# The first feed-forward product as seven block products of sums, in a hybrid diffusion block on one Trainium2 core

## The chip, the cores and the metric

One core of a Trainium2 chip runs the whole program once. The metric is the device time of that one execution in microseconds (us). Before the change it is 974.69 us, the median of 3 runs (974.1 to 976.0). The engines are TensorE (PE, with its weight loads shown as a row of its own, PEld), VectorE (DVE), ScalarE (ACT), GpSimd (POOL) and SyncE (SP), which here only issues transfers.

## The reference

One layer over 512 latent tokens of width 1024, with 256 context tokens. Three mixers run on the same normalised input, are merged by gates and projected back; then comes a SwiGLU feed-forward part with `D_FF = 2816`, and a last normalisation. The change concerns the product `h @ w_ffn_in`, of 512x1024 by 1024x5632.

```python
def swiglu(h, w_ffn_in, w_ffn_out):
    a, b = split_cols(h @ w_ffn_in, (D_FF, D_FF))
    return (jax.nn.silu(a) * b) @ w_ffn_out

x = x + g2 * swiglu(modulate(x, norm2_g[layer], sh2, sc2), w_ffn_in[layer], w_ffn_out[layer])
return rmsnorm(x, final_g)
```

## The kernel before

All products are done in a split form. An fp32 operand is rounded to fp32r on ACT (`A.copy`, L143) and the rest is taken on DVE (`V.tensor_tensor` subtract, L144); a product of two split operands is then three matmuls, high by high, high by low and low by high (`mm3`, L255 to L257). Every weight block of 128x1024 numbers (512 KB) is loaded by SP into one of three buffers `wf` (`load_w`, L139), and split into one of two buffer pairs `wh`, `wl` (`prep_w`). So a pair comes free only when the matmuls of two blocks earlier are done, and a buffer `wf` only when its split is done.

The order of each engine's instructions is fixed when the program is built: a scheduler takes the instructions by priority (weight loads and splits have the priority "prep", ahead of "main") and by its own estimate of when they can start. On the chip each engine runs its list strictly in that order, and waits at the first instruction whose inputs or buffers are not ready.

The last part of the kernel has three stages.

1. The product with `w_o` (`gemm_tm`, L985). It runs over token tiles m = 0 to 3 of 128 tokens, and as each tile's sums finish, the loop around it (L1028 and on) adds the residual (L1008), squares and sums (L1009), scales the row (L1030), transposes the tile in 8 blocks on PE (L1037), applies scale and shift (half of the blocks on DVE at L1043, half on ACT at L1041) and splits the result into `h2h`, `h2l`, features on partitions and tokens along the row. So the second normalisation of the last tiles lies beside the first matmuls of the next stage.
2. The first feed-forward product, 11 groups of 256 columns of `a` and the same 256 columns of `b`. Group 0 is done in two halves of 256 tokens, so that it can start before tokens 256 to 511 are there (192 matmuls of 256 columns). Groups 1 to 10 have 96 matmuls each, of 512 columns. `silu(a)` is done on ACT (L1082), the product with `b` on DVE (L1083), and the result is split at once into `Ga`, `Gb`.
3. The product with `w_ffn_out`, `gemm_tm` again over 22 blocks of 128 weight rows, each first multiplied by the gate `g2b` (L154), with the last normalisation behind it.

PSUM has eight banks of 512 fp32 columns: three `g`, one `t`, four `d`.

Of the kernel before, what the change touches and what calls it, by code (L numbers as in the profile page):

```python
# [9 lines left out]
F32 = mybir.dt.float32  # L10
# [64 lines left out]
def body(tc, I, out):  # L75
# [3 lines left out]
    with es:  # L79
# [22 lines left out]
        def gbank(name="g"):  # L102
            return psg.tile([128, 512], F32, name=name, tag="g")
# [708 lines left out]
        def cvf():  # L812
            return pF.tile([128, 512], F32, name="cvf", tag="cv", bufs=3)
# [212 lines left out]
        h2h = pH.tile([128, 8, 512], F32R, name="h2h", tag="hh")  # L1026
        h2l = pH.tile([128, 8, 512], F32R, name="h2l", tag="hl")
        for m, ps in gemm_tm(I["w_o"][0], g1b, lambda k, ms: (mh[:, k, ms], ml[:, k, ms]), 8, extra, 1):  # L1028
            rs_ = residual(ps, xr, m, [xn[:, m % 2, 512 * n:512 * n + 512] for n in range(2)])
            V.tensor_scalar(out=xn[:, m % 2], in0=xr[:, m], scalar1=rs_, scalar2=None, op0=ALU.mult)  # L1030
            for k4 in range(2):
                px = dbank()
                hf = cvf()
                p3, h3 = (t.rearrange("p (k j) -> p k j", k=4) for t in (px, hf))
# [9 lines left out]
                ms = slice(128 * m, 128 * m + 128)  # L1044
                split(h3, h2h[:, 4 * k4:4 * k4 + 4, ms], h2l[:, 4 * k4:4 * k4 + 4, ms])
        fstack.close()


        pG = es.enter_context(tc.tile_pool(name="pG", bufs=1))
        Ga = pG.tile([128, 18, 2, 512], F32R, name="Ga")  # L1050
        Gb = pM.tile([128, 4, 2, 512], F32R, name="Gb", tag="M16")
        Gt = [Ga[:, k] for k in range(18)] + [Gb[:, k] for k in range(4)]
        gw = pM.tile([128, 2, 2, 4, 256], F32R, name="gw", tag="C16")
        wfi = I["w_ffn_in"][0].rearrange("(k p) f -> p k f", p=128)
        H2 = (lambda k: h2h[:, k], lambda k: h2l[:, k], 512, gbank)
        cvg = lambda: pG.tile([128, 512], F32, name="cvg", tag="cv", bufs=3)
        for g in range(11):
            if g == 0:

                ab = [[gbank() for _ in range(2)], [gbank(), tbank()]]  # L1060
                wts = []
                for i in range(2):
                    for half in range(2):
                        dst = None
                        if i:
                            dst = [gw[:, half, p] for p in range(2)]
                        wts.append(prep_w(load_w(wfi[:, 4 * half:4 * half + 4, 2816 * i:2816 * i + 256]), dst=dst))
                for th in range(2):
                    ts = slice(256 * th, 256 * th + 256)
                    for i in range(2):  # L1070
                        for q in range(2):
                            cs = slice(128 * q, 128 * q + 128)
                            for k in range(8):
                                wh, wl = wts[2 * i + k // 4]
                                mm3(ab[i][q][:, ts], wh[:, k % 4, cs], wl[:, k % 4, cs], h2h[:, k, ts], h2l[:, k, ts], k == 0, k == 7)
                pa_, pb_ = ab
# [3 lines left out]
            for q in range(2):  # L1080
# [9 lines left out]
        for m, ps in gemm_tm(I["w_ffn_out"][0], g2b, lambda k, ms: (Gt[k][:, 0, ms], Gt[k][:, 1, ms]), 22, extra):  # L1090
            yo = yos[:, m]
            rs_ = residual(ps, xr, m, [cvg() for _ in range(2)])
# [19 lines left out]
```

## Time and profile before

| | before |
|---|---|
| median of 3 runs | 974.69 us |
| the profiled execution | 969.97 us, of it span 968.2 us |
| TensorE busy | 952.9 us, 98% of the span, 5964 matmuls |
| VectorE busy | 543.2 us, 56% |
| ScalarE busy | 421.8 us, 44% |
| GpSimd busy | 28.8 us, 3% |
| read from HBM | 110.58 MB, 118 GB/s over the span |

The profile is of one execution; its times are read as durations of single instructions and as the distance between the starts of neighbours. Matmuls are pipelined: one lasts longer than the distance to the next, so the distance between starts is what a matmul costs in a stream. A wait in brackets behind a row is the idle time of the engine ahead of it and what ended it.

### The profile page before, as it was taken

Reading aid. Unit: us, or ns where it says so; the run is one execution under the profiler, and the core shown is the slowest. Engines: PE = TensorE matmul, PEld = TensorE weight load, DVE = VectorE, ACT = ScalarE, POOL = GpSimd, SP = SyncE. Lnnn points to the kernel's source line nnn. Section 1 sums busy time; section 2 is a strip of 40 time slices with the busy share of each in tenths; the row PEclk is TensorE's granted clock in tenths of the full one; section 3 lists DMA queues with packets and bytes.
Section 4 is the critical chain, followed back from the end, with each engine's and each line's share of the span. In section 5 each row is a group of like instructions: output and inputs, shape, how many; then the busy total and the mean of one; then the engine's idle time right before and its main releaser. Section 6 shows DMA issues by size and latency. Waiting matters only on the chain.

```text
span 968.2 us, 14628 instructions
## 1 busy us (share of the span) xinstructions
PE 952.9 (98%) x5964; PEld 785.1 (81%) x5964; DVE 543.2 (56%) x880; ACT 421.8 (44%) x733; POOL 28.8 (3%) x47
## 2 busy tenths in 40 slices
PE   8999999999999999999999999999999999999997
PEld 7587888777888888888778888988888888888885
DVE  3575888379755333787874977333333333444455
ACT  5363985597773333362234346322323232311224
POOL 1002300000000000000000000000000000000000
PEclk9999999999999999999999999999999999999999
DMA  9820553421202323847765252223232332333322
GB/s 330 292 66 3 144 131 88 132 67 34 67 2 66 109 88 84 291 131 267 253 219 174 91 172 66 66 87 109 88 107 88 99 98 91 91 102 98 97 88 87
DMA packets 96836, 115.30 MB, mean 119 GB/s; under 512 B 18124, under 2 KB 84032, under 8 KB 96768
## 3 DMA queue, kind: packets, MB, share of 16 engines
q1 hardware_dynamic: 88192, 109.01, 35.7%
q0 software_dynamic: 1632, 3.44, 1.4%
q10 hardware_dynamic: 6944, 1.91, 0.8%
q8 instruction: 47, 0.77, 0.3%
q14 instruction: 21, 0.17, 0.1%
HBM read 110.58 MB, written 3.77 MB: 118 GB/s over the span
## 4 chain that ended last, share of the span: by engine, by line
PE 83%; DVE 6%; ACT 5%; DMA 4%; issue 2%; POOL 0%; SPq 0%; DVEq 0%; ACTq 0%
PE g L256 19%; PE g L257 19%; PE g L255 19%; PE d L255 5%; PE d L256 5%; PE d L257 5%; DMA wm<-in_w_mod_dram 2%; DVE acc L835 1%; DVE wl L144 1%; PE t L257 1%; PE t L255 1%; PE t L256 1%; PE d L238 1%; ACT TBD L639 1%; DMA acc<-in_b_mod_dram 1%
## 5 line engine op out<-in xcount | busy, mean ns | idle before, releaser
L144 DVE TENSOR_TENSOR wl<-wf,wh 128x1024 fp32r<-128x1024 f32 x131 | 160.1, 1222 | 205.0 <-ACT wh L143 204.1
L143 ACT CAST wh<-wf 128x1024 fp32r<-128x1024 f32 x131 | 137.8, 1052 | 309.9 <-PE g L256 169.6
L257 PE MATMUL g<-hh,wl 128*128 128x512 f32 x368 | 146.0, 397 | 0.3 <-DVE wl L144 0.3
L255 PE MATMUL g<-hh,wh 128*128 128x512 f32 x368 | 146.1, 397 | 0.0
L256 PE MATMUL g<-hl,wh 128*128 128x512 f32 x368 | 145.9, 396 | 0.0
L255 PE MATMUL g<-h2h,wh 128*128 128x512 f32 (+1 forms) x352 | 133.6, 380 | 0.0
L257 PE MATMUL g<-h2h,wl 128*128 128x512 f32 (+1 forms) x352 | 133.5, 380 | 0.0
L256 PE MATMUL g<-h2l,wh 128*128 128x512 f32 (+1 forms) x352 | 133.5, 379 | 0.0
L257 PEld LDWEIGHTS g<-hh,wl 128*128 128x128 f32 x368 | 69.6, 189 | 15.0 <-DVE wl L144 1.0
L256 PEld LDWEIGHTS g<-hl,wh 128*128 128x128 f32 x368 | 69.6, 189 | 13.7 <-issue 0.2
L255 PEld LDWEIGHTS g<-hh,wh 128*128 128x128 f32 x368 | 69.6, 189 | 13.6 <-issue 0.2
L255 PEld LDWEIGHTS g<-h2h,wh 128*128 128x128 f32 x352 | 66.2, 188 | 12.6
L256 PEld LDWEIGHTS g<-h2l,wh 128*128 128x128 f32 x352 | 66.2, 188 | 12.6
L257 PEld LDWEIGHTS g<-h2h,wl 128*128 128x128 f32 x352 | 66.1, 188 | 12.3
L154 DVE TENSOR_TENSOR wf<-wf,g2b 128x1024 f32<-128x1024 f32 x22 | 27.0, 1226 | 54.3 <-DMA wf<-in_w_ffn_out_dram 54.2
L835 DVE SCALAR_TENSOR_TENSOR acc<-wm,ct,acc 128x1024 f32<-128x1024 f32 x32 | 41.0, 1282 | 17.5 <-DMA acc<-in_b_mod_dram 8.0
L255 PE MATMUL d<-wh,Ga 128*128 128x512 f32 x72 | 28.0, 389 | 0.0
L256 PE MATMUL d<-wl,Ga 128*128 128x512 f32 x72 | 28.0, 389 | 0.0
L257 PE MATMUL d<-wh,Ga 128*128 128x512 f32 x72 | 28.0, 389 | 0.0
L718 ACT ACTIVATE SJ<-SJ,eGl 128x128 f32<-128x128 f32 x80 | 25.1, 402 | 3.8 <-PE d L706 2.6
L143 ACT CAST Ga<-cvg 128x512 fp32r<-128x512 f32 x18 | 11.1, 619 | 25.4 <-DVE cvg L1083 25.4
L616 DVE TENSOR_TENSOR t<-W 128x30 f32<-128x30 f32 (+29 forms) x60 | 19.3, 322 | 3.7 <-issue 2.7
(467 smaller groups left out, 1712.0 us busy)
## 6 DMA issues: line engine op xcount, KB each, us to landing
wm<-in_w_mod_dram SPq DMA_DIRECT2D x48, 512.0 KB, 5.3
wf<-in_w_ffn_in_dram SPq DMA_DIRECT2D x44, 512.0 KB, 3.5
wf<-in_w_in_dram SPq DMA_DIRECT2D x31, 512.0 KB, 3.9
wf<-in_w_gate_dram SPq DMA_DIRECT2D x24, 512.0 KB, 3.8
wf<-in_w_ffn_out_dram SPq DMA_DIRECT2D x22, 512.0 KB, 3.5
wf<-in_w_o_dram SPq DMA_DIRECT2D x8, 512.0 KB, 3.6
xl<-in_x_dram SPq DMA_DIRECT2D x4, 512.0 KB, 5.1
wf<-in_w_sc_out_dram SPq DMA_DIRECT2D x4, 512.0 KB, 3.3
```

Source lines behind the costliest of these rows:

```text
L143: A.copy(out=hi, in_=f)
L144: V.tensor_tensor(out=lo, in0=f, in1=hi.bitcast(F32), op=ALU.subtract)
L154: V.tensor_tensor(out=w, in0=w, in1=scale, op=ALU.mult)
L238: T.matmul(pm[32 * j:32 * j + 32, n * i:n * i + n], lhsT=ct[:, k, :], rhs=w[:, kk, :], start=k < 4, stop=k >= 4, tile_position=(0, 32 * j))
L255: T.matmul(ps, lhsT=lh, rhs=rh, start=start, stop=False)
L256: T.matmul(ps, lhsT=lh, rhs=rl, start=False, stop=False)
L257: T.matmul(ps, lhsT=ll, rhs=rh, start=False, stop=stop)
L616: V.tensor_tensor(out=t, in0=W3[0:n, j + 1:, j:j + 1].broadcast_to(sh_), in1=W3[0:n, j:j + 1, 0:j].broadcast_to(sh_), op=ALU.mult)
L639: A.copy(out=TBD[qs, slot, :, 32 * q:32 * q + 32], in_=Sy[qs])
L718: A.activation(out=S[:, u ^ par, h], in_=S[:, u ^ par, h], func=AF.Copy, scale=eGl[:, u, c_:c_ + 1])
L835: V.scalar_tensor_tensor(out=acc, in0=w, scalar=ct[:, k, 0:1], in1=acc, op0=ALU.mult, op1=ALU.add)
```

## The change

The 2x2 block product of a group of columns is done with seven products instead of eight. The weight of a group is cut into four blocks (`wsrc(i, half, g)`: i = 0 for `a`, 1 for `b`; half for features 0 to 511 and 512 to 1023), the tokens into two halves of 256. Seven sums of weight blocks meet seven sums of blocks of `h`, and the four results (`a` and `b`, for each half of the tokens) are sums of the products. The scheme of before had, in the same units, eight products.

- Each product (`prod`) is 24 matmuls of 256 columns: two column tiles, four feature blocks, three matmuls of the split form.
- The sums of `h` are made once, behind the second normalisation (`sums_b`, and `T4` at L1140), and are split like `h` before.
- The sums of weights are made for each group: one block is loaded by SP into a buffer of its own (`t` in `pre`, `w` in `ws`, two of each), a second block is added by a transfer of POOL's queue that accumulates into it (`acc_w`, L1113), and two more blocks are added on DVE (`add_w`, L1117). So a group issues seven transfers of 512 KB (five of SP, two of POOL) where it had four.
- In the groups a third split pair (`third`, shown as `w3`) is used in turn with `wh`, `wl`, so a split can start when the product of three places earlier is done (`prep3`).
- The results of a group are put together on DVE (`u2`, `e57`, `c22`, `c12`, `c21`, then two products with `silu`), with two copies and two `silu` on ACT. `G` is kept in fp32 (`Gq`), and split only when the second product comes to it (`g_of`).
- For groups 0 to 2 the two products that need only the first half of the tokens (`ahead` with `B11`, `ahead2` with `B21`) are put ahead of everything else, 144 matmuls in six products.

```diff
+        def prod(bank, w, b, first, last):
+            for q in range(2):
+                o, cs = bank[:, 256 * q:256 * q + 256], slice(128 * q, 128 * q + 128)
+                for kk in range(4):
+                    mm = ((w[0], b[:, 0]), (w[0], b[:, 1]), (w[1], b[:, 0]))
+                    for i, (l_, r_) in enumerate(mm):
+                        T.matmul(o, lhsT=l_[:, kk, cs], rhs=r_[:, kk], start=first and q == kk == i == 0,
+                                 stop=last and kk == 3 and i == 2, skip_group_check=True)
+        def acc_w(w, src):
+            with prio("prep"):
+                GP.dma_start(out=w, in_=src, accum_op=ALU.add)
+        def add_w(w, other):
+            with prio("prep"):
+                V.tensor_tensor(out=w, in0=w, in1=other, op=ALU.add)
...
+            for h, js in parts:
+                V.tensor_tensor(out=Bf[:, 0:4, js], in0=h[0], in1=Bf[:, 0:4, js], op=ALU.subtract)
+                split_b(Bf[:, 0:4, js], "T1", js)
...
+        def ahead(g, e):
+            X = gbank()
+            prod(X, prep_w(load_w(wsrc(0, 0, g))), OB["B11"], True, False)
+            A.copy(out=e, in_=X)
+            return X
+        def ahead2(g, X):
+            prod(X, prep_w(load_w(wsrc(0, 1, g))), OB["B21"], False, True)
...
+        EARLY = 3
+        Xs = [ahead(g, e1s[g]) for g in range(EARLY)]
+        for g in range(EARLY):
+            ahead2(g, Xs[g])
+        V.tensor_tensor(out=Bf[:, 4:8], in0=Bf[:, 4:8], in1=Bf[:, 0:4], op=ALU.subtract)
+        split_b(Bf[:, 4:8], "T4", slice(0, 256))
...
         for g in range(11):
-            if g == 0:
...
-                (pa_,) = gemm_fm(wfi[:, :, 256 * g:256 * g + 256], (H2,))
-                (pb_,) = gemm_fm(wfi[:, :, 2816 + 256 * g:2816 + 256 * g + 256], (H2,))
-            for q in range(2):
-                sa = cvg()
-                A.activation(out=sa, in_=pa_[q], func=AF.Silu)
-                V.tensor_tensor(out=sa, in0=pb_[q], in1=sa, op=ALU.mult)
-                split(sa, Gt[2 * g + q][:, 0], Gt[2 * g + q][:, 1])
+            t, w = pre[g % 2], ws[g % 2]
+            load_w2(wsrc(1, 0, g), t)
+            acc_w(t, wsrc(1, 1, g))
+            load_w2(wsrc(0, 0, g), w)
+            acc_w(w, wsrc(1, 0, g))
+            v = load_w(wsrc(0, 0, g))
+            if g < EARLY:
+                e1 = e1s[g]
             else:
+                X, e1 = gbank(), e1g
+                prod(X, prep3(v), OB["B11"], True, False)
+                A.copy(out=e1, in_=X)
+            bA = gbank()
+            prod(bA, prep3(t), OB["T1"], True, False)
+            A.copy(out=e5, in_=bA)
+            add_w(t, v)
+            bD = dbank()
+            prod(bD, prep3(t), OB["T2"], True, True)
+            V.tensor_tensor(out=u2, in0=bD, in1=e1, op=ALU.subtract)
+            bB = gbank()
+            prod(bB, prep3(w), OB["T3"], True, False)
+            V.tensor_tensor(out=e57, in0=bB, in1=e5, op=ALU.add)
+            V.tensor_tensor(out=c22, in0=u2, in1=e57, op=ALU.add)
+            a12 = load_w(wsrc(0, 1, g))
+            if g >= EARLY:
+                prod(X, prep3(a12), OB["B21"], False, True)
+                A.activation(out=Gq[g][:, :, 0:256], in_=q2(X), func=AF.Silu)
+            add_w(t, a12)
+            prod(bA, prep3(t), OB["nB22"], False, True)
+            V.tensor_tensor(out=c12, in0=u2, in1=bA, op=ALU.add)
+            A.activation(out=Gq[g][:, :, 256:512], in_=q2(c12), func=AF.Silu, scale=-1.0)
+            prod(bB, prep3(load_w(wsrc(1, 1, g))), OB["T4"], False, True)
+            V.tensor_tensor(out=c21, in0=u2, in1=bB, op=ALU.add)
+            for c_, cs in ((c22, slice(256, 512)), (c21, slice(0, 256))):
+                V.tensor_tensor(out=Gq[g][:, :, cs], in0=q2(c_), in1=Gq[g][:, :, cs], op=ALU.mult)
...
+                with prio("prep"):
+                    split(Gq[k // 2][:, k % 2], slot[:, 0], slot[:, 1])
```

In the order of PE, at the start of the first feed-forward product, the transposes of the last token tile (the rows with `xn`) stood before behind the 42nd matmul of group 0:

```order
L255 MATMUL g_5707<-h2h_5311,wh_5718 128x256
L256 MATMUL g_5707<-h2l_5312,wh_5718 128x256
L1037 MATMUL d_5675<-cp_82,xn_5310 128x128 x4
L1037 MATMUL d_5687<-cp_82,xn_5310 128x128 x4
L257 MATMUL g_5707<-h2h_5311,wl_5719 128x256
```

Now they stand behind the 24th, the last of the first product (bank `g_5735`, weight `wh_5738`); behind them comes the second product, with the weight `wh_5770`, `wl_5771`:

```order
L1108 MATMUL g_5735<-ob_5311,wh_5738 128x256 x2
L1108 MATMUL g_5735<-ob_5311,wl_5739 128x256
L1071 MATMUL d_5669<-cp_82,xn_5310 128x128 x4
L1071 MATMUL d_5679<-cp_82,xn_5310 128x128 x4
L1108 MATMUL g_5767<-ob_5311,wh_5770 128x256 x2
L1108 MATMUL g_5767<-ob_5311,wl_5771 128x256
```

So 18 matmuls fewer lie ahead of these transposes, and nothing but them between the first and the second product.

In the order of DVE at the same place, from the residual of the last token tile (`d_5320`) to the weight that follows, before:

```order
L1008 TENSOR_TENSOR xr_5300<-xr_5300,d_5320 128x512
L144 TENSOR_TENSOR wl_5719<-wf_5716,wh_5718 128x1024
L144 TENSOR_TENSOR h2l_5312<-cvf_5618,h2h_5311 128x4x128
L1010 TENSOR_TENSOR n_r_5666<-n_s_5665 128x1
L144 TENSOR_TENSOR h2l_5312<-cvf_5630,h2h_5311 128x4x128
L1012 RECIPROCAL n_r_5666<-n_r_5666 128x1
L1030 TENSOR_SCALAR xn_5310<-xr_5300,n_r_5666 128x1024
L1043 TENSOR_SCALAR cvf_5676<-d_5675,a2_3963,sh2_3964 128x128
```

And now, from the scaled row of the last tile to the third weight of the six products ahead (`obt` and `ob_5312` are the sums of `h`, split):

```order
L1061 TENSOR_SCALAR xn_5310<-xr_5300,n_r_5660 128x1024
L1047 TENSOR_TENSOR c16_5314<-h2f_5626,c16_5314 128x4x128
L144 TENSOR_TENSOR ob_5312<-tb_5701,ob_5312 128x4x128
L1077 TENSOR_SCALAR h2f_5670<-d_5669,a2_3963,sh2_3964 128x128
L1077 TENSOR_SCALAR h2f_5680<-d_5679,a2_3963,sh2_3964 128x128
L144 TENSOR_TENSOR obt_5313<-c16_5314,obt_5313 128x4x128
L1077 TENSOR_SCALAR h2f_5670<-d_5669,a2_3963,sh2_3964 128x128
L1077 TENSOR_SCALAR h2f_5680<-d_5679,a2_3963,sh2_3964 128x128
L144 TENSOR_TENSOR wl_5771<-wf_5768,wh_5770 128x1024
L1044 TENSOR_TENSOR c16_5314<-h2f_5670,c16_5314 128x4x128
L144 TENSOR_TENSOR wl_5803<-wf_5800,wh_5802 128x1024
```

The split of the second product's weight, `wl_5771`, now stands behind the scale and shift of the last tile and three pieces of the sums.

In the order of SP, now, at the same place: the first two loads into the new buffers `ws` stand ahead of the load of the sixth product's weight (`wf_5891`) and of the first group's `v` (`wf_5931`).

```order
L139 DMA wf_5831<-in_w_ffn_in_dram 128x4x256
L139 DMA wf_5861<-in_w_ffn_in_dram 128x4x256
L1121 DMA ws_5730<-in_w_ffn_in_dram 128x4x256
L1121 DMA ws_5731<-in_w_ffn_in_dram 128x4x256
L139 DMA wf_5891<-in_w_ffn_in_dram 128x4x256
L139 DMA wf_5931<-in_w_ffn_in_dram 128x4x256
```

Before, SP had only the loads `wf` in this stage, one behind the other.

## Rows read from the trace of the kernel before

**Rows 1.** The page: busy time by engine; shares of the chain that ended last.
```profile
PE 952.9 (98%) x5964; PEld 785.1 (81%) x5964; DVE 543.2 (56%) x880; ACT 421.8 (44%) x733; POOL 28.8 (3%) x47
...
PE 83%; DVE 6%; ACT 5%; DMA 4%; issue 2%; POOL 0%; SPq 0%; DVEq 0%; ACTq 0%
```

**Rows 2.** Busy by stretch: us, PE, PEld, DVE, ACT, POOL (instructions), PEclk, DMA, GB/s.
```profile
598.00:623.00 25.00, 25.00 (x206) 24.72 (x205) 12.05 (x21) 12.39 (x22) 0.00 (x0) 1.00 0.18 55
623.00:841.00 218.00, 218.00 (x965) 180.52 (x964) 77.80 (x82) 63.77 (x80) 0.54 (x1) 1.00 0.32 96
841.00:968.00 127.00, 119.91 (x528) 98.61 (x526) 61.97 (x67) 33.53 (x47) 0.00 (x0) 0.99 0.29 94
```

**Rows 3.** Timeline of PE, first feed-forward product: start us, length us, engine, line, names.
```profile
605.81 0.28 PE L255 MATMUL g<-h2h,gw 128*128 128x256 f32 x1
...
622.97 0.28 PE L257 MATMUL t<-h2h,gw 128*128 128x256 f32 x1
623.09 0.40 PE L255 MATMUL g<-h2h,wh 128*128 128x512 f32 x1
...
840.71 0.39 PE L255 MATMUL g<-wh,Ga 128*128 128x512 f32 x1
```

**Rows 4.** Groups by shape, 570 to 968 us: count | busy us, mean ns | idle.
```profile
L256 PEld LDWEIGHTS g<-h2l,wh 128*128 128x128 f32 x352 | 66.2, 188 | 12.6
...
L256 PE MATMUL g<-h2l,wh 128*128 128x256 f32 x32 | 9.0, 282 | 0.0
```

**Rows 5.** The same view, DVE and ACT of the last stages.
```profile
L144 DVE TENSOR_TENSOR wl<-wf,wh 128x1024 fp32r<-128x1024 f32 x63 | 77.0, 1223 | 129.2 <-ACT wh L143 129.0
L143 ACT CAST wh<-wf 128x1024 fp32r<-128x1024 f32 x63 | 66.2, 1053 | 183.8 <-PE d L257 73.3 <-PE g L256 72.9 <-issue 34.8
...
L154 DVE TENSOR_TENSOR wf<-wf,g2b 128x1024 f32<-128x1024 f32 x22 | 27.0, 1226 | 54.3 <-DMA wf<-in_w_ffn_out_dram 54.2
...
L1083 DVE TENSOR_TENSOR cvg<-g,cvg 128x512 f32<-128x512 f32 x21 | 14.5, 691 | 12.1 <-PE g L257 12.1
...
L1082 ACT ACTIVATE cvg<-g 128x512 f32<-128x512 f32 x22 | 13.1, 594 | 18.5 <-PE g L257 18.5
...
L144 DVE TENSOR_TENSOR h2l<-cvf,h2h 128x512 fp32r<-128x512 f32 x8 | 5.3, 688 | 1.4 <-ACT h2h L143 1.3
```

**Rows 6.** Timeline at the start of the first feed-forward product, PE and DVE.
```profile
598.79 0.39 PE L257 MATMUL d<-wh,ml 128*128 128x512 f32 x1
599.02 0.28 PE L255 MATMUL g<-h2h,wh 128*128 128x256 f32 x1
...
599.39 0.68 DVE L1008 TENSOR_TENSOR xr<-xr,d 128x512 f32<-128x512 f32 x1
...
603.23 0.75 DVE L1030 TENSOR_SCALAR xn<-xr,n_r 128x1024 f32<-128x1024 f32 x1
...
604.09 1.04 PE L1037 MATMUL d<-cp,xn 128*128 128x128 f32 x8
604.74 1.79 DVE L1043 TENSOR_SCALAR cvf<-d,a,sh 128x128 f32<-128x128 f32 x4 [0.75 <-PE d L1037]
```

**Rows 7.** Transfers: issuing queue, count, KB each, median us from issue to landing.
```profile
wf<-in_w_ffn_in_dram SPq DMA_DIRECT2D x44, 512.0 KB, 3.5
...
ET<-Gdn POOLq DMA_DIRECT2D x8, 128.0 KB, 8.3
...
fgb<-in_final_g_dram POOLq DMA_DIRECT2D x1, 512.0 KB, 4.0
```

**Rows 8.** Busy by stretch as above: where the granted clock (PEclk) was low.
```profile
84.00:86.00 2.00, 2.00 (x13) 1.58 (x6) 0.50 (x4) 1.53 (x2) 0.00 (x0) 0.51 0.00 0
86.00:88.00 2.00, 2.00 (x7) 1.61 (x6) 1.76 (x8) 0.00 (x0) 0.00 (x0) 0.64 0.00 0
...
965.00:966.00 1.00, 0.00 (x0) 0.00 (x0) 0.00 (x0) 0.00 (x0) 0.00 (x0) 0.50 0.92 348
```

**Rows 9.** Timeline of PE in the first stretch of rows 8.
```profile
84.64 0.63 PE L257 MATMUL g<-hh,wl 128*128 128x512 f32 x1
85.07 0.63 PE L255 MATMUL g<-hh,wh 128*128 128x512 f32 x1
```

**Rows 10.** Timeline of PE in the last blocks of the second feed-forward product.
```profile
941.54 0.50 PE L256 MATMUL g<-wl,Gb 128*128 128x512 f32 x1 [0.23 <-DVE wl L144]
```

More of the change, by code (lines that the diff above doesn't have):

```diff
@@ L1030, in body @@
             V.tensor_scalar(out=xn[:, m % 2], in0=xr[:, m], scalar1=rs_, scalar2=None, op0=ALU.mult)
+            js = slice(128 * (m % 2), 128 * (m % 2) + 128)
+            hs = []
             for k4 in range(2):
                 px = dbank()
-                hf = cvf()
-                p3, h3 = (t.rearrange("p (k j) -> p k j", k=4) for t in (px, hf))
+                p3 = px.rearrange("p (k j) -> p k j", k=4)
+                h3 = Bf[:, 4 * k4:4 * k4 + 4, js] if m < 2 else pF.tile([128, 512], F32, name="h2f", tag=("u", "gt")[m - 2], bufs=2).rearrange("p (k j) -> p k j", k=4)
+                hs.append(h3)
                 for kk in range(4):
@@ L1043, in body @@
                         V.tensor_scalar(out=h3[:, kk], in0=p3[:, kk], scalar1=a2[:, k:k + 1], scalar2=sh2[:, k:k + 1], op0=ALU.mult, op1=ALU.add)
-                ms = slice(128 * m, 128 * m + 128)
-                split(h3, h2h[:, 4 * k4:4 * k4 + 4, ms], h2l[:, 4 * k4:4 * k4 + 4, ms])
+                if m < 2:
+                    split_b(h3, ("B11", "B21")[k4], js)
+            if m == 2:
+                hs2 = hs
+            elif m == 3:
+                sums_b(((hs2, slice(0, 128)), (hs, slice(128, 256))))
@@ new lines, in body @@
+        OB["T4"] = pG.tile([128, 2, 4, 256], F32R, name="ob4")
+        tmps = pG.tile([128, 7, 512], F32, name="tmps")
+        e1g, e5, u2, e57, c22, c21, c12 = (tmps[:, i] for i in range(7))
+        Gq = [pG.tile([128, 2, 512], F32, name="Gq", tag=f"Gq{i}") for i in range(11)]
+        ws = [pG.tile([128, 4, 256], F32, name="ws", tag=f"ws{i}") for i in range(2)]
+        third = [pG.tile([128, 4, 256], F32R, name="w3", tag=f"w3{i}") for i in range(2)]
+        turn = itertools.count()
+        prep3 = lambda w_: prep_w(w_, dst=third if next(turn) % 3 == 2 else None)
@@ new lines, in acc_w, with load_w2 @@
+        def acc_w(w, src):
[4 more added lines that the diff above has]
+                V.tensor_tensor(out=w, in0=w, in1=other, op=ALU.add)
+        def load_w2(src, w):
+            with prio("prep"):
+                SY.dma_start(out=w, in_=src)
+            return w
+        def ahead(g, e):
[3 more added lines that the diff above has]
+            return X
@@ new lines, in body @@
+        q2 = lambda t_: t_.rearrange("p (q j) -> p q j", q=2)
+        for g in range(EARLY):
+            A.activation(out=Gq[g][:, :, 0:256], in_=q2(Xs[g]), func=AF.Silu)
+        for g in range(11):
+            t, w = pre[g % 2], ws[g % 2]
[6 more added lines that the diff above has]
+                e1 = e1s[g]
+            else:
+                X, e1 = gbank(), e1g
[24 more added lines that the diff above has]
+                V.tensor_tensor(out=Gq[g][:, :, cs], in0=q2(c_), in1=Gq[g][:, :, cs], op=ALU.mult)
@@ L1085, in body, with g_of @@
+        gs = pM.tile([128, 4, 2, 512], F32R, name="gs", tag="M16")
+        halves_g = {}
+        def g_of(k, ms):
+            slot = gs[:, k % 4]
+            if k not in halves_g:
+                halves_g[k] = True
+                with prio("prep"):
+                    split(Gq[k // 2][:, k % 2], slot[:, 0], slot[:, 1])
+            return slot[:, 0, ms], slot[:, 1, ms]
         fgb = pM.tile([128, 1024], F32, name="fgb", tag="C16")
@@ L1089, in body @@
         extra = [(ex[:, i, 0], ex[:, i, 1]) for i in range(2)]
-        for m, ps in gemm_tm(I["w_ffn_out"][0], g2b, lambda k, ms: (Gt[k][:, 0, ms], Gt[k][:, 1, ms]), 22, extra):
+        for m, ps in gemm_tm(I["w_ffn_out"][0], g2b, g_of, 22, extra):
             yo = yos[:, m]
-            rs_ = residual(ps, xr, m, [cvg() for _ in range(2)])
+            rs_ = residual(ps, xr, m, [tmps[:, 2 * (m % 2) + i] for i in range(2)])
             V.tensor_tensor(out=yo, in0=xr[:, m], in1=fgb, op=ALU.mult)
```

51 lines of the change are left out of this document (26 added, 25 removed).

## The prediction

> **What bounds the kernel now.** I read the page's busy times and chain first. PE is busy for 98% of the span and makes up 83% of the chain that ended last [rows 1]. Then the stretches by stage: in the first feed-forward product (599 to 841 us) PE is busy all the time at the full clock, while DVE has 77.8 of 218 us and ACT 63.8 [rows 2]. So PE sets this stage, and fewer PE cycles shorten it as long as the other engines keep up. Last I read the timeline of PE for what one matmul costs in a stream, and the start of the stage, where DVE and ACT are in front of PE.
>
> **PE: removed and added.** From 605.81 to 622.97 lie 143 steps of 256-column matmuls, each with a weight load of its own: 17.16 / 143 = 0.120 us. From 623.09 to 840.71 lie 960 of 512 columns: 217.62 / 960 = 0.2267 us [rows 3]. Half the columns thus cost 53%, not 50%: about 13 ns of each matmul do not shrink. Before: 192 x 0.120 + 960 x 0.2267 = 240.7 us. Now: 11 groups x 7 products x 24 = 1848 matmuls x 0.120 = 221.8 us. PE alone saves 18.9 us; an eighth would be 30, and the 13 ns take the difference.
>
> A weight load has a row of 188 ns, longer than the 0.120 us between two matmuls [rows 3, 4]. The loads overlap each other and the matmuls, and did so 144 times in a row without a gap.
> The Trainium skill ("TensorE: Matmul & The Clock Gate", section Part 3, "What overlaps and what doesn't") says that a weight load overlaps running matmuls only where it goes to another row group, and these all use the full array. By that rule, with the 107 ns that its section on LDWEIGHTS gives for 128 columns, a pair would cost some 213 ns, and 1848 of them 394 us (an estimate from the page). The trace disagrees, with 120 ns per pair, so the sum goes by the trace.
>
> **DVE, ACT in a group.** Per group DVE does 7 splits x 1.223, 2 weight additions x 1.226 and 7 operations of 512 columns x 0.691 [rows 5] = 15.9 us, beside 7 x 24 x 0.120 = 20.2 us of PE. ACT: 7 x 1.053 + 4 x 0.594 = 9.7 us [rows 5]. A split can start when the product three places earlier is done, so it has two products (5.8 us) for 1.05 + 1.22 = 2.3 us: it stays hidden, with some 3 us for what stands ahead of it in DVE's order (one or two combinations that wait for a bank, 0.69 each). In groups 0 to 2 it is 13.4 us of DVE to 14.4 us of PE: hidden too, but with little to spare. I take nothing for either; if the cover fails by 1 us in each group, that is 11 us.
>
> **Transfers in a group.** Seven of 512 KB in 20.2 us are 182 GB/s, where 96 ran before [rows 2]. A plain load lands in 3.5 us [rows 7]. No accumulating transfer stands in the trace. The nearest rows are POOL's: 4.0 us for 512 KB and 8.3 us for 128 KB in small pieces [rows 7]. The bounds are 4 and 8.3, or more if it is slow in itself; I take 6, nearer to the row of equal size, since it also has to read what it adds to. A buffer `t` comes free at the sixth product of the group two before, and is wanted split by the second product of this one: ten products, 29 us, less 3.5 for the load and 2.3 for the split. Up to some 20 us an accumulation costs nothing in the later groups. In group 0 it is on the edge (below).
>
> **The start of the stage,** where I find the whole cost. The first product needs only tokens 0 to 255 and starts at 599.0 as before; it takes 24 x 0.120 = 2.9 us, to 601.9. Then PE's order has the transposes of the last token tile, and these need its scaled rows. Before, DVE had these at 603.23 + 0.75 = 604.0 [rows 6], after 2.6 us of splits behind the residual; now it has two subtractions, one negation and one split there, 4 x 0.69 = 2.8 us. So they come at 604.1, and PE waits 2.2 us where 42 matmuls covered it before. The transposes take 1.0, to 605.2. The next product needs `wl_5771`, and DVE first does a subtraction and a split (1.4), the scale and shift (1.79 [rows 6]) with another split in between (0.7), then the weight split (1.22): 604.1 + 5.1 = 609.2. PE waits 3.8, after two matmuls that need the high part only. The next two products last until 614.7. DVE meanwhile does six pieces of sums (6 x 0.69), one of 1024 columns (1.22) and two weight splits (2.4), to 617: 2.2 us of wait. The sixth product's weight can be loaded only when a buffer is split at 617; it lands at 620.5, and cast and split end at 622.8, while PE is there at 622.3; the first matmuls of group 0 stand inside this product and want a high part that ACT casts behind it: 1 us. The second of group 0 is late by about 0.4, if its neighbour in DVE's order, the split of the accumulated `ws`, has landed by 624.7. Its load can start when the old pool is free, at 614.6, lands at 618.5, and with 6 us for the accumulation it is just there; with 8.3 it costs 2 us. From then on the splits are ahead of PE. Sum: 2.2 + 3.8 + 2.2 + 1.0 + 0.4 = 9.6 us. From below: the first two waits go if the normalisation of the last tile runs 2 us faster beside this order, which leaves about 4. From above: 2 for a late `ws`, and the clock.
>
> The granted clock fell to 1.2 GHz in two places: at 84 to 87 us, after a run of very small matmuls, and at the kernel's end, with no matmul left [rows 8]. At that level matmuls of 512 columns came 0.43 us apart instead of 0.227 (84.64, 85.07 [rows 9]), for eight of them: 1.6 us lost. My longest waits are 3.8 and 2.2 us with a few matmuls between, so I keep 2 us for it in the range, none in the sum.
>
> **The second product** takes over the 22 splits of `G`: 22 x 0.69 on DVE beside 127 us where it has 62 [rows 2, 5]. They fit (3.1 us per block to 5.4 of PE), except at the entry, where the first weight's split stands behind three pieces (0.3 us), and in the last block, where PE already waits 0.23 us [rows 10] and one more cast goes first (0.3 us). 0.6 us in all.
>
> **Sum.** -18.9 + 9.6 + 0.6 = -8.7 us. The profiled execution took 969.97, so 961.3; it lies 0.5% under the median of the runs shown, 974.69. The same -0.9% from the median gives 966 us.
>
> **Rivals.**
> - *The start costs less* (a wait that I add up is covered). For it: the scheduler set this order by its own estimate of when rows are there, and the transposes are placed as if the wait were short. Against: DVE's row of operations after the residual is as long as before. At 4 us and below: 974.7 - 18.9 + 4 + 0.6, some 960, down to 956.
> - *PE starves further.* DVE at 93% in groups 0 to 2, a late `ws`, a low clock, or 1 us per group. Price 4 to 11 us over the sum: 970 to 977, a small gain to a small loss.
> - *The accumulating transfers become the bound: slower.* Place: POOL's queue, two of them per group, 22 in all. For it: the trace has none, POOL's small-piece row is 8.3 us for a quarter of the bytes [rows 7], and all that PE does behind a `t` or `w` hangs on them. Against: POOL's row of 512 KB lands like SP's. If they pass one after another, it decides from 10 us each (two in 20.2 us). At 12 us a group lasts 24: 11 x 3.8 = 42 us on top of the sum, 1008; at 20 us, 1180.
> - *The 256-column matmul goes at the pace of its weight load: slower.* At the row's 188 ns [rows 4], 1848 x 0.188 = 347 us, 107 more than now: about 1090 us. The 144 steps of rows 3 speak against it. It is also what the Trainium skill's rule above comes to.
>
> **Chances and range.** Measurements of this kernel tell a change from none at about 0.2%, 2 us. Forecast (960 to 972): 0.62. A cheaper start: 0.12. Starved further: 0.14, of which 0.04 still faster, 0.06 the same, 0.04 slower. Accumulation as the bound: 0.10. Weight loads: 0.02. Faster 0.78, same 0.06, slower 0.16. The range of 957 to 974 leaves out some 0.03 below and 0.16 above.
>
> **What would show it.** Right: neighbours of 256 columns 0.120 us apart through groups 3 to 10, a group about 20.2 us long; PE idle some 10 us between 599 and 630, longest ahead of the last tile's transposes and of the second product, ended by DVE's scaled rows and `wl`; DVE near 80% in the groups. Wrong: DVE or ACT waiting for `ws` or `c16` from POOL's transfers in every group; more than 0.13 us between matmuls; a granted clock at half in the groups; PE idle in each group, ended by a split.

## The result and the profile after

The changed kernel took 964.6 us (961.5 to 966.2, four runs) beside 974.7 for the kernel before: ratio 0.9891, 95% interval 0.9864 to 0.9918. In a second comparison it took 964.4 beside 971.3: 0.9924 (0.9906 to 0.9941). It is faster, and 966 was forecast. Its profiled execution took 965.04 us, where the sum had 961.3.

The page of the kernel after: busy time by engine, and shares of the chain that ended last.

```profile
PE 939.9 (98%) x6660; PEld 807.7 (84%) x6660; DVE 649.3 (67%) x1002; ACT 467.9 (49%) x793; POOL 57.2 (6%) x69
...
PE 76%; DVE 9%; DMA 6%; ACT 6%; issue 2%; POOL 0%; SPq 0%; DVEq 0%; ACTq 0%
```

PE is busy for 13 us less than in [rows 1], not 18.9, in part because a matmul at half the clock counts as busy for longer. It has a smaller share of the chain: DVE, DMA and ACT have more of it. Where, the stretches say (columns as in [rows 2]).

```profile
598.50:640.00 41.50, 34.22 (x235) 32.13 (x234) 29.72 (x40) 24.44 (x39) 3.85 (x3) 0.88 0.64 164
640.00:835.20 195.20, 195.20 (x1629) 195.20 (x1628) 155.22 (x167) 90.39 (x108) 22.37 (x18) 1.00 0.74 181
835.20:963.20 128.00, 120.43 (x530) 98.77 (x528) 75.22 (x87) 42.50 (x64) 0.00 (x0) 0.99 0.31 95
```

From 640 us on PE is busy all the time at the full clock. Before that it idles 7 of 41 us, and the clock is at 0.88. PE's timeline has both ends of the first product, two matmuls in a group, and every wait at the start in brackets.

```profile
599.26 0.40 PE L1108 MATMUL g<-ob,wh 128*128 128x256 f32 x2
...
603.54 1.06 PE L1071 MATMUL d<-cp,xn 128*128 128x128 f32 x8 [1.25 <-DVE xn L1061]
606.74 0.80 PE L1108 MATMUL g<-ob,wh 128*128 128x256 f32 x2 [2.14 <-ACT wh L143]
608.00 0.58 PE L1108 MATMUL g<-ob,wl 128*128 128x256 f32 x1 [0.46 <-DVE wl L144]
...
616.77 0.50 PE L1108 MATMUL g<-ob,wh 128*128 128x256 f32 x2 [0.82 <-ACT wh L143]
623.42 0.51 PE L1108 MATMUL g<-ob,wh 128*128 128x256 f32 x2 [0.85 <-ACT wh L143]
624.36 0.51 PE L1108 MATMUL g<-obt,wh 128*128 128x256 f32 x2 [0.44 <-ACT wh L143]
631.24 0.50 PE L1108 MATMUL d<-obt,wh 128*128 128x256 f32 x2 [1.03 <-ACT wh L143]
631.99 0.47 PE L1108 MATMUL g<-ob,w 128*128 128x256 f32 x2 [0.24 <-issue]
...
700.20 0.40 PE L1108 MATMUL d<-obt,wh 128*128 128x256 f32 x2
...
701.64 0.40 PE L1108 MATMUL d<-obt,wh 128*128 128x256 f32 x2
...
835.20 0.40 PE L255 MATMUL g<-wh,gs 128*128 128x512 f32 x1
```

Between 700.20 and 701.64 lie four times three matmuls: 0.120 us each, as forecast. The product lasts from 599.26 to 835.20, 235.9 us, where [rows 3, 6] had 599.02 to 840.71, 241.7. Of the 235.9, 221.8 are matmuls and 1.06 the last tile's transposes; the start cost the other 13.1, not 9.6. The eight waits add up to 7.2. Five of them end with a high part cast on ACT. ACT stood for 3.50 us ahead of a copy that needs the end of the second product, and the casts that PE waits for next come behind that copy:

```profile
612.87 0.59 ACT L1128 COPY e<-g 128x512 f32<-128x512 f32 x1 [3.50 <-PE g L1108]
```

The stretches with a low clock (PEclk, the third number from the right) hold more:

```profile
604.00:608.00 4.00, 1.40 (x8) 0.87 (x6) 3.75 (x8) 3.67 (x7) 0.00 (x0) 0.70 0.00 0
608.00:612.00 4.00, 4.00 (x18) 4.00 (x19) 4.00 (x6) 1.37 (x3) 0.00 (x0) 0.50 0.58 172
...
632.00:636.00 4.00, 3.96 (x20) 3.75 (x21) 2.80 (x3) 1.04 (x1) 1.27 (x1) 0.61 0.62 180
```

The granted clock fell to 1.2 GHz behind the waits of 1.25 and 2.14 us, and again behind the one of 1.03. One minus PEclk, times PE's busy time, over these stretches and the two behind them (0.95 and 0.96) gives 4.3 us. Some 1.6 us have no row.

The chain of waits shows what is behind the second fall (start us, us, what).

```profile
615.26 4.14 DMA ws<-in_w_ffn_in_dram
619.40 0.10 issue
619.50 7.09 DMA ws<-in_w_ffn_in_dram
626.59 0.02 issue
626.61 1.05 ACT w L143
...
628.84 1.23 DVE c L1117
...
630.14 1.05 ACT wh L143
```

Group 0's second weight sum is a plain load and an accumulating one of 7.09 us; its split stands on DVE ahead of the addition for the next product, and PE waits for that. The page has the accumulating transfers (POOLq) beside plain ones (KB each, median us to landing):

```profile
c<-in_w_ffn_in_dram POOLq DMA_DIRECT2D x11, 512.0 KB, 6.6
ws<-in_w_ffn_in_dram POOLq DMA_DIRECT2D x11, 512.0 KB, 7.9
...
ws<-in_w_ffn_in_dram SPq DMA_DIRECT2D x11, 512.0 KB, 3.8
```

In the later groups they are hidden. The first combination that reads the second sum's product (`u2`, L1164) follows itself by 20.16 us, which is 168 x 0.120, in each of the last seven groups:

```profile
682.76 0.69 DVE L1164 TENSOR_TENSOR tmps<-d,tmps 128x512 f32<-128x512 f32 x1 [0.65 <-PE d L1108]
...
702.92 0.69 DVE L1164 TENSOR_TENSOR tmps<-d,tmps 128x512 f32<-128x512 f32 x1 [0.65 <-PE d L1108]
```

### The profile page after: what moved, and what is told of

Its sections match the earlier page's. It is cut to its first block, busy times and chain, and to the rows that moved or that the text cites. A ratio compares the mean times of both kernels' runs of the same rounds, so it can differ in the third digit from the quotient of the medians.

```text
span 963.2 us, 16357 instructions
## 1 busy us (share of the span) xinstructions
PE 939.9 (98%) x6660; PEld 807.7 (84%) x6660; DVE 649.3 (67%) x1002; ACT 467.9 (49%) x793; POOL 57.2 (6%) x69
## 4 chain that ended last, share of the span: by engine, by line
PE 76%; DVE 9%; DMA 6%; ACT 6%; issue 2%; POOL 0%; SPq 0%; DVEq 0%; ACTq 0%
PE g L1108 17%; PE g L256 10%; PE g L257 10%; PE g L255 10%; PE d L256 5%; PE d L255 5%; PE d L257 5%; PE d L1108 3%; DVE wl L144 2%; DMA wm<-in_w_mod_dram 2%; DMA ws<-in_w_ffn_in_dram 1%; DVE acc L835 1%; DMA wf<-in_w_o_dram 1%; ACT wh L143 1%; ACT SJ L718 1%
## 5 line engine op out<-in xcount | busy, mean ns | idle before, releaser
L144 DVE TENSOR_TENSOR wl<-wf,wh 128x1024 fp32r<-128x1024 f32 x114 | 139.1, 1222 | 93.1 <-ACT wh L143 92.2
L1108 PE MATMUL g<-ob,wh 128*128 128x256 f32 x640 | 118.7, 287 | 3.8 <-ACT wh L143 3.8
L1108 PEld LDWEIGHTS g<-ob,wh 128*128 128x128 f32 x640 | 101.6, 195 | 4.5 <-ACT wh L143 4.5
L1108 PE MATMUL g<-ob,wl 128*128 128x256 f32 x320 | 91.6, 287 | 0.5 <-DVE wl L144 0.5
L1108 PEld LDWEIGHTS g<-ob,wl 128*128 128x128 f32 x320 | 62.3, 195 | 0.8 <-DVE wl L144 0.8
L1108 PE MATMUL g<-ob,w 128*128 128x256 f32 x360 | 45.9, 283 | 0.2 <-issue 0.2
L1108 PEld LDWEIGHTS g<-ob,w 128*128 128x128 f32 x360 | 44.3, 192 | 0.4 <-issue 0.4
L143 ACT CAST wh<-c 128x1024 fp32r<-128x1024 f32 x21 | 22.0, 1048 | 37.0 <-DVE c L1117 19.5
L255 PE MATMUL d<-wh,gs 128*128 128x512 f32 x80 | 31.1, 389 | 0.0
L257 PE MATMUL d<-wh,gs 128*128 128x512 f32 x80 | 31.1, 389 | 0.0
L256 PE MATMUL d<-wl,gs 128*128 128x512 f32 x80 | 31.1, 389 | 0.0
```

Of the source, the lines that this page charges most:

```text
L143: A.copy(out=hi, in_=f)
L144: V.tensor_tensor(out=lo, in0=f, in1=hi.bitcast(F32), op=ALU.subtract)
L255: T.matmul(ps, lhsT=lh, rhs=rh, start=start, stop=False)
L256: T.matmul(ps, lhsT=lh, rhs=rl, start=False, stop=False)
L257: T.matmul(ps, lhsT=ll, rhs=rh, start=False, stop=stop)
L1108: T.matmul(o, lhsT=l_[:, kk, cs], rhs=r_[:, kk], start=first and q == kk == i == 0, stop=last and kk == 3 and i == 2, skip_group_check=True)
```

## Experiments

Executions of one kernel differ by some us in the stages ahead of this change (see the first experiment). So beside each time stand two lengths of its profiled execution. The stretch goes from the last `w_dn_out` block (the last start in the row of its `g<-ydn,wh` matmuls, 551.2 in the kernel after) to the first matmul of the second product (835.20): 284.0 us. Of this, 47.5 to 49.0 us lie ahead of the first product, so some of that spread is still in it. The product goes from its own first matmul to the same end: 235.9 us. Last stand PE's waits in the product, added up (those over 0.15 us), and what the low clock took there (one minus PEclk, times PE's busy time, for each microsecond).

| kernel | us | ratio to before (95%) | stretch | product | waits + clock |
|---|---|---|---|---|---|
| before, two profiles | 971.3 | 1 | 289.3, 289.6 | 241.7, 241.7 | 0, 0 |
| changed, two profiles | 964.4 | 0.9924 (0.9906 to 0.9941) | 284.0, 284.1 | 235.9, 235.2 | 7.2 + 4.3, 7.7 + 3.1 |
| before_256 | 985.7 | 1.0147 (1.0133 to 1.0162) | 302.1 | 254.5 | 0 |
| two_pairs | 969.6 | 0.9986 (0.9972 to 1.0000) | 288.5 | 241.0 | 11.3 + 3.1 |
| plain_second | 961.3 | 0.9899 (0.9875 to 0.9923) | 279.2 | 231.8 | 5.7 + 1.5 |
| sums_whole | 964.1 | 0.9931 (0.9915 to 0.9947) | 285.3 | 237.8 | 8.9 + 4.4 |
| sums_late | 960.9 | 0.9893 (0.9880 to 0.9906) | 281.7 | 234.2 | 7.3 + 3.4 |
| swap | 966.0 | 0.9951 (0.9934 to 0.9967) | 283.4 | 235.9 | 8.4 + 3.2 |
| late_swap | 958.1 | 0.9865 (0.9843 to 0.9887) | 279.4 | 231.0 | 4.1 + 3.4 |
| late_x2 | 960.4 | 0.9890 (0.9869 to 0.9912) | 279.1 | 230.1 | 4.7 + 1.6 |
| late_x3 | 962.8 | 0.9921 (0.9901 to 0.9940) | 280.6 | 232.5 | 7.4 + 1.5 |
| late_pool | 964.5 | 0.9929 (0.9908 to 0.9950) | 284.0 | 235.7 | 7.6 + 4.4 |

The theory: PE sets the product, which gains 18.9 us, and the start gives back what DVE, ACT and a late buffer keep PE waiting there, with a low clock behind it. The rivals: the accumulating transfers cost time in every group; the amount of vector work, and not its order, makes the start.

**The two kernels again.** No edit.

> The kernel before once more, for a second profile. Its profiled execution of the prediction was 969.97 us where its timed ones were 974 to 976 and, in later comparisons, 969 to 976. If the spread lies in the feed-forward stage, this profile shows another length there than 241.7 us; if it lies ahead of it, the stage has 241.7 us again and its start moves.

> The changed kernel once more, against the kernel before in five rounds, for a narrower ratio and a second profile. The theory (TensorE sets the feed-forward stage: 2,112 steps of 0.120 us fewer than its steps of before are worth, minus the waits and the low clock at the stage's start) expects 10 us less than before, 0.990 (0.988 to 0.992), and the same seven waits behind the last token tile, 1.0 to 2.2 us each at most, with a granted clock of 0.5 for some 4 us behind them. A rival that puts part of the gain down to chance of the runs expects a ratio nearer to 0.995, as the two profiled executions alone (969.97 and 965.04) say.

PE's timeline in the second profile of the kernel before, whose execution took 973.14 us:

```profile
602.26 0.28 PE L255 MATMUL g<-h2h,wh 128*128 128x256 f32 x1
...
843.95 0.39 PE L255 MATMUL g<-wh,Ga 128*128 128x512 f32 x1
```

241.7 us again, 3.2 us later: the spread lies ahead of the product. The changed kernel has 235.2 in its second profile, the waits 1.25, 2.14 and 0.76 in the same place, then 0.82, 0.55, 1.85 and 0.33. But the granted clock did not do the same. It fell behind the first waits only, and stayed up behind the one of 1.85 us, where the first profile had it at 0.61 behind one of 1.03:

```profile
608.00:612.00 4.00, 3.24 (x16) 3.23 (x16) 4.00 (x6) 2.14 (x4) 0.00 (x0) 0.52 0.44 136
612.00:616.00 4.00, 4.00 (x24) 4.00 (x24) 1.86 (x4) 2.13 (x4) 0.00 (x0) 0.63 0.39 126
...
632.00:636.00 4.00, 2.93 (x20) 2.60 (x21) 2.45 (x2) 1.88 (x3) 1.27 (x1) 1.00 0.77 249
```

So what the clock takes differs by 1.2 us between two executions of one kernel, and a difference of that size between two kernels is not yet an effect of their edits. In the stretch the change is worth 5.3 and 5.5 us. The medians say 6.9 here and 10.1 in the first comparison, where the kernel before had 974.7 against 970.6 to 971.7 in all later ones. The ratio 0.9924 lies a little outside the 0.988 to 0.992 that were expected (its interval reaches into them), halfway between 0.990 and the rival's 0.995. (The 2,112 steps in the expectation are the kernel before, counted in steps of 256 columns; the changed kernel has 1,848.)

**Half the columns, the same arithmetic** (before_256).

```diff
-  one matmul of 512 columns: rhs=h2h[:, k]
+  for ts in (slice(0, 256), slice(256, 512)): matmul into ps[q][:, ts], rhs=h2h[:, k, ts]
```

> The kernel before, with the 960 matmuls of 512 columns in its groups 1 to 10 of the first feed-forward product each done as two of 256 columns; the arithmetic, the weights and the splits stay. The theory reads a fixed 13 ns in each step (0.120 us against half of 0.2267) and expects 960 x (2 x 0.120 - 0.2267) = 12.8 us more: 987 us, 1.013. If a 256-column step were free of a fixed cost, it would be 974.7; if the weight load of 188 ns a matmul stood beside no other matmul, far above 1,050.

14.4 us slower in the medians, 12.7 in the stretch (302.1 to 289.4), where 12.8 was expected. The fixed 13 ns of a matmul is shown by itself, and that a weight load of 188 ns for each does not set the pace: 640 rows of each kind follow each other like these.

```profile
700.02 0.28 PE L1067 MATMUL g<-h2h,wh 128*128 128x256 f32 x1
700.14 0.28 PE L1067 MATMUL g<-h2l,wh 128*128 128x256 f32 x1
```

**Without the third pair** (two_pairs).

```diff
- prep3 = lambda w_: prep_w(w_, dst=third if next(turn) % 3 == 2 else None)
+ prep3 = lambda w_: prep_w(w_, dst=None)
```

> The changed kernel without its third pair of split-weight buffers: every product uses the two pairs that the kernel has elsewhere. A pair is free at the end of one product and wanted again after the next, 2.88 us later; cast and split take 1.05 + 1.22 us with a gap or two, some 2.4 us if both engines are free at once, and VectorE is busy for 80% of a group. The theory (the third pair is what keeps the products back to back) expects waits of 0.3 to 1 us at a third to all of the 74 products, partly with the low clock behind them: 972 to 1,010 us. A rival by which 2.4 is less than 2.88 and the pair was not needed expects 964 to 966.

5.2 us slower than the changed kernel, under every number expected of the theory and over the rival's. A group takes 20.72 us, 0.56 more, and in each PE waits 0.3 to 0.5 us for DVE, where it did not wait (once, in the last group, 1.4 us). PE's waits from 640 to 840 us (us in total, times, longest), then DVE's timeline:

```profile
PE d L1108 <- DVE wl L144: 3.4, 10, 0.5
PE g L1108 <- DVE tmps L1167: 1.4, 1, 1.4
```

```profile
684.35 0.69 DVE L1164 TENSOR_TENSOR tmps<-d,tmps 128x512 f32<-128x512 f32 x1 [0.60 <-PE d L1108]
...
705.07 0.69 DVE L1164 TENSOR_TENSOR tmps<-d,tmps 128x512 f32<-128x512 f32 x1 [0.60 <-PE d L1108]
```

Most splits are hidden with two pairs as well. What the third pair is worth is still three quarters of the change's 6.9 us.

**Plain transfers instead of accumulating ones** (plain_second).

```diff
- GP.dma_start(out=w, in_=src, accum_op=ALU.add)
+ GP.dma_start(out=w, in_=src)
```

> The changed kernel with the transfers that add to a weight buffer done as plain ones of the same size on the same queue, so the addition of the first half of each of those sums is left out. The theory (the accumulating transfers are hidden in the groups, and near the path in group 0 alone) expects 0.5 to 2.5 us less, all of it between 615 and 640 us, and groups of 20.2 us as before: 962 to 964. The rival by which accumulating sets the pace expects shorter groups and 5 us less or more.

3.2 us faster, 4.8 in the stretch, 3.4 to 4.2 in the product; the time is a little under what was expected. From group 2 on the pace is the same, 20.16, so the rival fell. Group 0's `u2` starts at 633.64 instead of 636.93, and no wait stands there. The waits are 1.5 to 2.0 us shorter than in the two profiles of the changed kernel, as expected, and all of them lie before 640. The rest is clock, 1.6 to 2.8 us, and not the accumulation's price alone: the fall behind the first waits, ahead of group 0, took 2.6 and 3.1 us there and 1.5 here. Nor does the edit explain the stage ahead (from `w_dn_out` to the first product), 47.5 us here and 48.1 and 48.9 in the changed kernel: two_pairs accumulates too and has 47.5.

**The sums made once** (sums_whole; `h22` are two tiles of 256 tokens, in `g1b` and in group 1's half of C16).

```diff
- h3 = ... pF.tile([128, 512], F32, name="h2f", tag=("u", "gt")[m - 2], bufs=2)
+ h3 = ... h22[k4][:, :, js]
- if m == 2: hs2 = hs
- elif m == 3: sums_b(((hs2, slice(0, 128)), (hs, slice(128, 256))))
+ if m == 3: sums_b(((h22, slice(0, 256)),))
```

> The activation's sums T1, T2, T3 and the negated block are made once, 256 tokens wide, after the last token tile, and no longer a token tile at a time; nothing else is changed. The order theory (waits at the start come from vector instructions that stand in front of the ones TensorE waits for) expects that the 1.25 us wait of the last tile's transposes goes, since no sum can now stand before the last tile's scaled rows, and that the 2.1 us wait of the second product stays or grows, since in the written order three sums of 1.22 us now stand right before the second weight half's low part: 962 to 965 us, against 964.6. A rival (the amount of vector work at the start decides, not its order) expects 0.6 us less work to be worth 0.6 us: 964; a third (the weights come too late from HBM) expects no change in any wait.

The transposes' wait fell from 1.25 to 0.27 us and the next one grew from 2.14 to 3.96, as the order said. The time is the same by the medians; the product is 2 us longer.

**And behind the second weight's split** (sums_late).

```diff
+ pre2 = [prep_w(load_w(wsrc(0, 0, g))) for g in range(2)]
+ with tc.issue_after(last_lo[0].ins):
      sums_b(((h22, slice(0, 256)),))
```

> As the kernel with the sums made once and 256 tokens wide, and the second weight half's split is ordered in front of the first sum on VectorE. The order theory expects both the 1.25 us and the 2.1 and 0.5 us waits to go, and with them the stretch of some 8 us at a granted clock of 0.5 to 0.7 behind them (worth some 3 us); what is left is the amount of vector work before the first group, so waits of 0.5 to 2 us in front of the groups' first products: 957 to 961 us, against 964.6. The rival by the amount of work expects 963 to 964, the rival by late weights 964 to 965 with the waits unchanged.

3.5 us faster than the changed kernel, at the upper end of what was expected. The waits up to 608 are 0.52 and 0.95, and PE runs at the full clock to 620. Then it stands:

```profile
626.31 0.77 PE L1111 MATMUL g<-ob,w 128*128 128x256 f32 x2 [5.21 <-issue]
```

```profile
615.48 9.66 DMA ws<-in_w_ffn_in_dram
```

```profile
624.00:628.00 4.00, 1.07 (x3) 0.81 (x4) 1.76 (x2) 2.83 (x4) 1.27 (x1) 0.50 1.18 238
628.00:632.00 4.00, 4.00 (x20) 4.00 (x20) 2.96 (x3) 1.04 (x2) 0.00 (x0) 0.50 1.17 245
```

PE's timeline, the chain of waits and the stretches: PE came early and met the accumulating transfer of group 0, 9.66 us beside the other loads, and the clock fell behind the wait. One cover was taken off the next wait: the waits add up to 7.3 us, as much as in the changed kernel. So of the 3.5 us only 1.0 to 1.7 lie in the product.

**Other buffers for group 0's sums** (swap).

```diff
- t, w = pre[g % 2], ws[g % 2]
+ t, w = ws if g % 2 else pre
```

> The changed kernel with its four buffers for the two accumulated weight sums dealt out otherwise: in even groups both sums take the two halves of C16, which are free long before the stage, in odd groups the two buffers of the late pool, which open only when the last token tile is done; nothing else is changed. In the changed kernel group 0's second sum waits for that pool: its plain load is issued at 615, its accumulating one at 619.5, and TensorE's third product of the group (w) waits for it. The theory (the sum's transfer is on the path in group 0 alone, by where its buffer lies) expects the waits of 0.9 to 1.0 us at 623 to 631 and the low clock at 632 to go, those at 603 to 608 to stay: 961 to 963.5 us against 964.4. A rival by which the accumulating transfers are slow everywhere expects no change (964), one by which VectorE's work at the start decides expects the wait to pass from the DMA to VectorE (963.5 to 964.5).

No gain. The waits at 631 went, and 1.35 and 0.75 us came at 637.88 and 639.13, in front of group 0's fourth product. The chain of waits has the reason:

```profile
625.20 10.17 DMA wf<-in_w_ffn_in_dram
...
635.46 1.24 DVE c L1117
```

A plain load of 512 KB, on which the addition for that product hangs, took 10.17 us instead of the 4.8 that is its median, beside the loads and accumulations for group 1, which started when the pool opened. So the wait moved from the pool's buffer to another transfer; no expectation named that. That the traffic beside it made this transfer slow is argued from the times, not tested.

**Both** (late_swap: sums_late, swap, and `gt`'s two buffers as one tile for `h22`).

> The kernel with the sums made once and behind the second weight's split, with the buffers dealt out as in the other kernel of this call (both sums of even groups in C16), so that group 0's second sum no longer waits for the late pool; two scratch buffers of an earlier stage share one tile to make room. In the kernel without this, TensorE waited 5.2 us for the accumulating transfer (issued 615.48, landed 625.14) and 1.0, 0.6 and 0.5 us elsewhere. The theory (order and buffer place, not amounts) expects the 5.2 us and the low clock behind it to go: 953 to 956 us against 960.9. The rival by the amount of vector work (some 18 us of it against 17.3 us of products before the first group's) expects half of it back as waits for VectorE: 957 to 959; if transfers are the bound in the groups too, 960 to 961.

958.1 us, 2.8 less than sums_late, and the fastest of all by the medians. It is in the range of the rival by amount (957 to 959), above the theory's: the 5.2 us went, but another wait came, for a copy into the late pool, where the rival had expected one for DVE:

```profile
619.30 0.50 PE L1112 MATMUL g<-ob,wh 128*128 128x256 f32 x2 [2.49 <-ACT tmps L1132]
```

**Two more orders** (late_x2, late_x3).

```diff
  prod(bA, prep3(t), OB["T1"], True, False)
+ if g == 0: ahead2(2, Xs[2])        # late_x2 and late_x3, no longer ahead of group 0
+ pre3 = [prep_w(load_w(wsrc(0, 0, g))) for g in range(3)]    # late_x3, ahead of h2f and the sums
```

> As the kernel with the late sums and both of an even group's weight sums in C16, with the second half of group 2's early product (and the Silu of it) moved behind group 0's first product. In that kernel TensorE's longest wait left is 2.5 us at 619.3, for the copy of group 2's first half into the late pool, which opens only when the negated block has been read from its old place; 4 us at a granted clock of 0.59 follow it, and 1.5 us of other waits stand at 605 to 607. The theory (what the order at the start puts in front of TensorE's next product decides) expects 2.5 us and up to 1.6 us of clock back: 954 to 956 us against 958.1. The rival by which VectorE's work at the start is itself the bound expects the wait to pass to group 0's products: 957 to 958.

> As the last one, and the third weight half of the stage is cast and split in front of the last token tile's activation on ScalarE and of the first sum on VectorE, where it waited for both before (0.5 and 1.0 us at 605 to 607). The theory expects these 1.5 us and the low clock behind them back: 952 to 955 us, 1 to 3 less than without it. The rival by VectorE's amount of work expects the same time as without it, with the wait in front of group 0's first product.

Neither gained: 960.4 and 962.8, with stretches of 279.1 and 280.6. The early waits of late_x3 shrank to 0.27, and the wait for the pool became 3.2 and 6.9 us. By the product, 230.1 us, late_x2 is 0.9 shorter than late_swap, but its waits are longer and only the clock took less. In all three the copy comes behind DVE's last read of `h22` (the negated block, L1062), which ended 19.6, 18.1 and 21.4 us after the product's first matmul, in late_x2 with two casts of ACT between. That order gains nothing here is what the rival by amount said; its times (957 to 958) and its place for the wait (group 0's products) were not met either, so the amount of vector work is not shown to be the cause.

**Three of the sums' instructions on GpSimd** (late_pool).

```diff
- V.tensor_tensor(out=t3, in0=h[0], in1=h[1], op=ALU.subtract)
+ GP.tensor_tensor(out=t3, in0=h[0], in1=h[1], op=ALU.subtract)
  (and the low parts of T3 and of the negated block)
```

> As the kernel with the late sums and both of an even group's weight sums in C16, with the sum T3, its low part and the negated block's low part (3 of the 7 vector instructions of the sums, 1.22 us each) done on GpSimd, which is idle there, and a sign change of 1 us more on ScalarE. Two kernels that changed only the order at the start (960.4 and 962.8 us) got nothing more: the wait at 619 to 624 became 3.2 and 6.9 us, always for the late pool, which opens when the negated block has been read. The theory as it now stands (behind the first two products it is the amount of vector work, some 13 us of it before that pool opens, that decides) expects 3.7 us less of it to open the pool that much sooner: the 2.5 us wait goes, 954 to 956 us against 958.1. If GpSimd takes over twice VectorE's time for these, or holds VectorE up, the pool opens as late as before or later: 958 to 962.

Slower by 6.4 us than late_swap, and above every time expected: PE waits 4.62 us at 619.00 for a `wl`. The timelines of POOL and of DVE:

```profile
610.13 3.32 POOL L1047 TENSOR_TENSOR ob<-h2f,ob 128x1024 fp32r<-128x1024 f32 x1 [1.16 <-ACT ob L1046]
613.41 3.32 POOL L1067 TENSOR_TENSOR ob<-h2f,ob 128x1024 fp32r<-128x1024 f32 x1
```

```profile
611.11 3.42 DVE L1058 TENSOR_TENSOR c<-h2f,c 128x1024 f32<-128x1024 f32 x1
614.57 3.25 DVE L1149 TENSOR_TENSOR c<-c 128x1024 f32<-128x1024 f32 x1
617.74 1.21 DVE L146 TENSOR_TENSOR wl<-wf,wh 128x1024 fp32r<-128x1024 f32 x1
```

Each DVE instruction begun beside one of POOL's ends 1.1 us after it, and 1.21 is what it takes alone: by these times it did not run slower, it stood until POOL was done. So this tells nothing on the amount of work: three instructions moved away held up three others by 2.1 us each. The rival by amount stays open.

## Why the prediction was right, and where its sum was not

- **-18.9 us for PE: right.** 0.120 us a matmul, 20.16 us a group, no wait of PE from 640 to 835. before_256 gives the fixed part by itself. The weight-load rival fell with it, and accumulation as the bound with the 20.16.
- **DVE and ACT hidden in the groups: right.** DVE has 155 of 195 us, 80%. A split needed less cover than the two products' time that was written: with one product's time (two_pairs) a group lost 0.56 us.
- **The waits at the start: right in place, 7.2 us (7.7 in the second profile) instead of 9.6, and partly for another engine.** For the transposes 1.25 (forecast 2.2), for the second product 2.14 + 0.46 (3.8), for the fourth 0.82 (2.2), for the sixth and group 0's first 0.85 + 0.44 (1.0), for group 0's second and third 1.03 + 0.24 (0.4). The forecast put the second product's and the fourth's down to `wl` on DVE; there PE waited first for the high part, cast on ACT, whose list the forecast followed in one place only.
- **"None in the sum" for the clock: the step that failed.** It was kept in the range at 2 us and cost 4.3 us in one profile and 3.1 in the other. [Rows 8, 9] gave the price of a step at half the clock, but no fall behind a wait; the one wait of over 1 us in the middle of that trace (1.33 us, at 242.0) had the clock at 1.00 behind it. In the changed kernel the steps behind the first waits came 0.21 us apart instead of 0.120 (three from 608.38 to 609.02).
- **`ws` "just there" with 6 us: on the wrong side.** It took 7.09 us, and 9.66 in sums_late. plain_second puts all accumulation at 1.5 to 2.0 us of waits, and what the clock took behind them.
- **The second product, 0.6 us:** 128.0 and 127.2 against 127.5 and 127.4. Not to be told from none.
- **The median.** In the product -5.8 and -6.5 us were measured where the same terms give -9.3. That 966 came so near the 964.6 is in part luck and rests on a second error: it was scaled to 974.7, and the kernel before has some 971 in four later comparisons. Against that, 966 would be a change of 5 us, near the 5.3 to 6.9 that stretch and medians give now. Why the first comparison had the kernel before 3 us higher stays open; the two profiles only place such spread ahead of the product.

What would give the rest is half shown: late_swap has 4.6 us of the 13 back in the stretch, by order and buffer place. Of what is left its largest wait, 2.5 us, hangs on a pool that opens only when the last vector instruction on the activation has read the old one; no run shows the time without it.

## What to carry to other kernels

Price a wait of PE at its length, and keep room for what the clock may take behind it: here 7.2 us of waits brought 4.3 more in one execution, and 7.7 brought 3.1 in another. Ahead of a new stage, list what each engine, and not only the one with the most work, has queued before the first thing the bottleneck needs, and which buffers lie in memory that the old stage still reads: a transfer can be late by where its buffer lies. And when one wait is removed, look for the next one under its cover before counting the gain: sums_late took away some 3 us of waits and met one of 5.2.

## What the runs showed of the hardware that was not expected

- The same waits did not always bring the low clock. Four kernels have the same two waits of 0.52 and 0.95 us at the start. Behind them the granted clock fell in late_swap and late_pool, and stayed at 1.00 in sums_late and late_x2. The stretch behind them in late_swap, then in sums_late:

```profile
608.00:612.00 4.00, 4.00 (x26) 4.00 (x26) 3.16 (x3) 2.92 (x4) 0.00 (x0) 0.69 0.79 256
```

```profile
608.00:612.00 4.00, 4.00 (x36) 4.00 (x35) 3.93 (x4) 3.47 (x5) 0.00 (x0) 1.00 0.76 253
```

- A VectorE instruction with both operands in SBUF stood still while GpSimd ran a `tensor_tensor`: 3.25 to 3.42 us instead of 1.22, ended 1.1 us after GpSimd's. The Trainium skill ("SBUF — State Buffer", section "Who interferes with whom") says so: with both inputs in SBUF such an instruction contends with GpSimd's reads, and the second to issue is blocked until the first is done. This trace agrees for VectorE's three; GpSimd's two that began while a VectorE instruction was under way took 3.32 us, the other one 3.22, so a block the other way does not show here.
- A transfer that adds to SBUF lands 6.6 to 7.9 us after its issue for 512 KB (medians of the changed kernel's two kinds), the plain one on the same queue (plain_second) 4.0 to 5.2.
